# Moving most SBUF tiles of a transformer trunk by 320 bytes, so that matmul operands agree modulo 512

## The chip, the cores and the metric

The kernel runs on one NeuronCore of a Trainium2 chip. The metric is the device time of one execution, in microseconds (us).

## What is computed

The reference is a two-layer decoder trunk over 256 tokens of 2048 features in float32. Layer 0 is a gated DeltaNet block and a squared-ReLU MLP; layer 1 is a differential attention on one shared K/V and a second MLP; each sub-layer ends in `x <- LayerNorm(4**0.25 * x + f(x))`. Cut to what matters here:

```python
D_MODEL, SEQ, D_FF = 2048, 256, 8192

def sq_relu_mlp(x, w_up, w_down):
    return jnp.square(jax.nn.relu(x @ w_up)) @ w_down

def gated_deltanet(x, w_in, conv_w, a_log, dt_bias, norm_w, w_out):
    p = x @ w_in                       # q, k, v, z and two gates
    ...
    return o.reshape(B, S, GDN_V_WIDTH) @ w_out

def diff_attention(x, w_q, lam_params, subln_w, w_o, k_sh, v_sh, lambda_init):
    q = (x @ w_q).reshape(...)
    ...
    return o.transpose(0, 2, 1, 3).reshape(B, S, DIFF_V_WIDTH) @ w_o
```

Nearly all the arithmetic is in the dense products with `w_in`, `w_out`, `w_kv`, `w_q`, `w_o`, `w_up` and `w_down`.

## The kernel before

**The products.** Each dense product is cut into products of 1024 output columns (`gemm`, L117); there are 50 of them. The activations are the stationary operand of TensorE and the weights stream past as the moving operand. Both are split into two parts, hi and lo, kept as float32r, and three passes (hi*hi, hi*lo, lo*hi) give a float32 result. `product` (L166) issues them: for a k-tile of 128 features and a token tile of 128 tokens, on each of two groups of 512 columns, L174 takes `xh` with `wh`, L175 `xh` with `wl`, L176 `xl` with `wh`. A product over 2048 features has 16 k-tiles, 2 token tiles and 2 column groups, so 192 matmuls of 128x128 (stationary) on 128x512 (moving). Each matmul has its own weight load (LDWEIGHTS) of the stationary part.

**Where the stationary operand lies.** Two families. In 30 of the 50 products (all of `w_in`, `w_up`, `w_kv`, `w_q`) it is the features of x in the constant tile `xhl` [128, 2, 2, 16, 128], made at L61 and read by `x_stat` (L110). In the 20 others (`w_out`, `w_down`, `w_o`) it lies in buffers of the pool `blk`, [128, 2048], read by `act_stat` (L114). A stationary part is 128 float32r, 512 bytes in a partition, and all of them follow each other without gaps, so that all parts of a tile start at the same place modulo 512 bytes as the tile. The same holds for the moving parts, 2048 bytes each, in buffers of 4096.

**Weights.** `load_weights` (L154) loads a k-tile of weights by a DMA of SP's queue into `wr`, ScalarE copies it to `wh` (rounded, L78), VectorE subtracts to get `wl` (L79). It runs ahead of TensorE through pools of 4 raw, 6 hi and 6 lo buffers.

**Between the products.** Evacuations, convolutions, the delta rule, attention scores and norms are emitted in units between groups of products (`later`, `soon`, `pump`, L178 to L194). Their transposes to the feature layout (`transpose4`, L200, matmuls of L204 with the identity `ident`) come in groups of four between the products' matmuls. In the DeltaNet stage (products 1 to 8) VectorE carries most of this work.

**Memory.** Constants come first in SBUF, then the pools in the order of L49 to L54 (`raw`, `hi`, `lo`, `blk`, `sm`, `tiny`). One constant, the convolution's taps `cw` (L380), lies behind `ident`, `xhl`, `mask`, `head_w`, `g_after`, `g_ones` and `g_col1` and ahead of `g_beta`, `g_g`, `nlam` and of all the pools.

Of the kernel before, what the change touches and what calls it, by code (L numbers as in the profile page):

```python
# [10 lines left out]
F32 = mybir.dt.float32  # L11
F32R = mybir.dt.float32r
# [6 lines left out]
P = 128  # L19
T = 256  # L20
# [15 lines left out]
class Trunk:  # L36
    """Products run with the activations as the stationary operand and the weights streaming past them.

    Both operands are split exactly into two parts of 12 significant bits (float32r); three passes,
    hi*hi + hi*lo + lo*hi, give a float32 product. Activations for a product are kept with the features  # L40
    on the partitions, [128, (hi, lo), token tile, k-tile, token]; everything else is [token, feature].
    """
# [38 lines left out]
    def rsqrt(self, dst, x, shape):  # L81
        """dst = x ** -0.5 for x > 0 (float32 accuracy: a guess from the exponent and three Newton steps)."""
        v = self.nc.vector
        y, t = self.small(shape, "rsq_y"), self.small(shape, "rsq_t")
        v.tensor_scalar(y.bitcast(I32), x.bitcast(I32), -0.5, float(0x5F3759DF), op0=ALU.mult, op1=ALU.add)
        for i in range(3):
            v.tensor_tensor(t, y, y, op=ALU.mult)
            v.scalar_tensor_tensor(t, t, -0.5, x, op0=ALU.mult, op1=ALU.mult)
            v.scalar_tensor_tensor(dst if i == 2 else y, t, 1.5, y, op0=ALU.add, op1=ALU.mult)

    def rsqrt_column(self, dst, x):
        """rsqrt of a column [128, 1] in fewer steps: (y y x - 3) y, Newton's step less its factor -1/2.

        The guess is scaled by a with -8192 a^27 = 1, which the three factors left out multiply back to 1.
        """
        v = self.nc.vector
        y, t = self.small([1], "rsq_y1"), self.small([1], "rsq_t1")
        a = -(8192.0 ** (-1.0 / 27.0))
        guess = RSQRT_GUESS - 2.0**31
        v.tensor_scalar(y.bitcast(I32), x.bitcast(I32), -0.5, guess, op0=ALU.mult, op1=ALU.add)  # L100
        for i, c in enumerate((3 * a**2, 12 * a**6, 768 * a**18)):
            v.scalar_tensor_tensor(t, y, x, y, op0=ALU.mult, op1=ALU.mult)
            last = v.scalar_tensor_tensor(dst if i == 2 else y, t, c, y, op0=ALU.subtract, op1=ALU.mult)
        return last

    def after(self, ins):
        """What is traced inside takes its turn on the engine of ins behind it."""
        return self.tc.issue_after(ins.ins) if ins is not None else nullcontext()
# [8 lines left out]
    def gemm(self, nk, wsrc, stat, evac, pre=None, rate=1, need=None, cuts=None):  # L117
        """Plans a product: evac(g, t, psum) gets out[token tile t, columns g * 512 ..] of the 1024 columns of wsrc(k)."""
        self.plan.append((nk, wsrc, stat, evac, pre, rate, need, cuts or [SC] * (nk // SC)))

    def run(self):
        steps = [(i, sum(gm[7][:n]), c) for i, gm in enumerate(self.plan) for n, c in enumerate(gm[7])]
        loaded, self.hold = {}, None
        self.load_weights(loaded, *steps[0])
        acc = {}
        for j, (i, s, n) in enumerate(steps):
            nk, _, stat, evac, pre, rate, need, _ = self.plan[i]
            if s == 0:
                acc = {}
                if pre is not None:  # L130
                    pre()
            if need is not None:
                need(s)
            ws = loaded.pop((i, s))
            for t in range(NT):
                # at the end of the second token tile one bank is done before the other, and evacuated meanwhile
                turns = [(g,) for g in range(NG)] if s + n >= nk and t == NT - 1 else [range(NG)]
                for gs in turns:
                    for n_, (k, wh, wl) in enumerate(ws):
                        self.product(acc, k, nk, t, gs, wh, wl, stat)  # L140
                        if n_ and self.pending:
                            fn, args = self.pending.popleft()
                            with self.after(self.last):
                                fn(*args)
                    if s + n >= nk:
                        for g in gs:
                            evac(g, t, acc[g, t])
                if t == 0 and j + 1 < len(steps):
                    with self.after(self.hold):
                        self.load_weights(loaded, *steps[j + 1], self.hold is not None)  # L150
                    self.hold = None
                self.pump(rate)
# [25 lines left out]
    def later(self, fn, *args):  # L178
        """Work on the side of the products: emitted between them, a unit at a time."""
        self.units.append((fn, args))  # L180

    def soon(self, fn, *args):
        """A step of an evac that the tensor engine takes a few products later, when its operand is ready."""
        self.pending.append((fn, args))

    def pump(self, n):
        """Emits n units, and one of the slow chain, whose steps wait for transfers."""
        if self.chain:
            fn, args = self.chain.popleft()
            fn(*args)  # L190
        while n > 0 and self.units:
            fn, args = self.units.popleft()
            fn(*args)
            n -= 1  # L194
# [5 lines left out]
    def transpose4(self, src):  # L200
        """[128, 512] -> PSUM [128, 4, 128], each 128 x 128 block transposed."""
# [5 lines left out]
    def to_features(self, src, dst, t):  # L207
        """src [128 tokens, 512] -> dst [128 features, (hi, lo), token tile, 4, 128 tokens] at token tile t."""
# [17 lines left out]
    def load_x(self, x):  # L226
        """The features of x by quarters: the first at once, the others between the first products."""
# [44 lines left out]
    def ln_finish(self, ln, t, own):  # L272
        """The last normalisation of a token tile: chunks below own on DVE, the others on ACT and Pool beside it."""
# [13 lines left out]
    def residual(self, n, alpha, ln=None):  # L287
        """The evac that adds a product's columns n * 1024 .. to the residual, and normalises it after the last."""
# [26 lines left out]
    def ends(n):  # L315
        """Before a normalisation the first token tile ends early, so that its rows are ready when the second ends."""
        return [5, 5, 6] if n == D // C - 1 else None

    def project_out(self, w, act, g, b, pre=None, need=None, out=None):
        """residual <- LayerNorm(alpha * residual + act @ w)."""  # L320
# [44 lines left out]
    def gated_deltanet(self, x, w_in, conv_w, a_log, dt_bias, norm_w, w_out, g, b, out=None):  # L365
        """The delta rule over all 256 tokens at once, two blocks of 128.

        With k2 = 2 k etc. (silu(y) = (tanh(y / 2) + 1) y / 2), S = |k2|^2 + 4 eps and c = beta / S:
        M = I + strict((k2 k2^T) c_j decay_ij), M y = v sqrt(S) / 2, o = 2 |q2|^-1 dk^-1/2 tril((q2 k2^T) c_j decay_ij) y.
        Matrices are kept transposed, [j, i]; the inverses of M's diagonal blocks are built from 32 x 32 ones.  # L370
        """
# [4 lines left out]
        mask = self.mask  # t <= i  # L376
        after = one.tile([P, P], F32R, name="g_after")  # t > j
        ones = one.tile([P, P], F32R, name="g_ones")
        col1 = one.tile([P, 1], F32, name="g_col1")
        cw = one.tile([P, 4 * 48], F32, name="g_cw")  # L380
# [28 lines left out]
        def gates():  # L409
            """beta = sigmoid(b), g = -exp(a_log) softplus(a + dt_bias) in two parts."""  # L410
# [6 lines left out]
            # the 32 columns four times over: float32r takes a stationary operand of 128  # L417
# [29 lines left out]
            # log(1 + e) = 2 atanh(e / (2 + e))  # L447
# [14 lines left out]
        def conv(raw, h, ct, dst):  # L462
            """Causal convolution and 2 silu of heads h, h + 1 of raw [channel, head, token] to dst [channel, 2, token]."""
# [48 lines left out]
        def score(hf, H, h):  # L512
            """U = (k k^T) c decay and A = (q k^T) c decay of heads h, h + 1, transposed."""
# [43 lines left out]
        def inv_gather(hf):  # L557
            """The 64 diagonal 32 x 32 blocks of the half, one to a partition."""
# [43 lines left out]
        def inv_merge(hf):  # L602
            """Y = the transposed inverses of the 16 128 x 128 blocks, from 32 to 64 to 128."""
# [28 lines left out]
        def solve(hf, gi, H):  # L632
            """Four heads: y, then o and its norm with the norm's weight (the gate follows with z)."""
# [124 lines left out]
    def diff_attention(self, w_kv, w_q, lam_params, subln_w, w_o, g, b, out=None):  # L758
# [27 lines left out]
        def heads(name, follow=None):  # L786
            """The evac that puts a product's heads with the features on the partitions: [128, head, token]."""
# [15 lines left out]
        def prob(hh, h, t, kb):  # L803
            """Where the transposed probabilities of a head's blocks lie: (0, 0), (1, 0), (1, 1)."""
# [3 lines left out]
        def score(kT, qT, hh, h, t):  # L808
            """Heads h, h + 1 of a half, query tile t; the two row tiles of a score go to banks of their own."""
# [40 lines left out]
        def values(hh, gi, t, v):  # L850
            """Four heads: probabilities @ v, the norm of each head, and the features for w_o."""
# [101 lines left out]
```

## Time and profile before

| | before |
|---|---|
| median of 3 runs | 2486.94 us |
| lowest and highest | 2485.38 and 2495.18 us |
| span of the profiled execution (first to last instruction) | 2493.5 us |
| TensorE busy, weight loads busy | 2448.1 us (98%), 1985.4 us (80%) |
| VectorE, ScalarE busy | 1498.4 us (60%), 1078.3 us (43%) |
| DMA | 438.84 MB, mean 176 GB/s |

The profile's page gives the span of the profiled execution and no time beside it. The span is 6.6 us above the median of the runs; of the three runs only the slowest, 2495.18 us, is longer than the span, by 1.7 us.

How to read it: PE is TensorE's matmuls and PEld its weight loads, DVE is VectorE, ACT ScalarE, POOL GpSimd, SP SyncE. A matmul's recorded duration runs from its start to its modelled end and overlaps the next one's, so the distance between two starts is the measure of the pace of the engine, and a row's mean duration is not. [...]

### The profile page before, as it was taken

Reading aid. Unit: us, or ns where it says so; the run is one execution under the profiler, and the core shown is the slowest. Engines: PE = TensorE matmul, PEld = TensorE weight load, DVE = VectorE, ACT = ScalarE, POOL = GpSimd, SP = SyncE. Lnnn points to the kernel's source line nnn. Section 1 sums busy time; section 2 is a strip of 40 time slices with the busy share of each in tenths; the row PEclk is TensorE's granted clock in tenths of the full one; section 3 lists DMA queues with packets and bytes.
Section 4 is the critical chain, followed back from the end, with each engine's and each line's share of the span. In section 5 each row is a group of like instructions: output and inputs, shape, how many; then the busy total and the mean of one; then the engine's idle time right before and its main releaser. Section 6 shows DMA issues by size and latency. Waiting matters only on the chain.

```text
span 2493.5 us, 30465 instructions
## 1 busy us (share of the span) xinstructions
PE 2448.1 (98%) x11492; PEld 1985.4 (80%) x11492; DVE 1498.4 (60%) x2333; ACT 1078.3 (43%) x1474; POOL 89.3 (4%) x94
## 2 busy tenths in 40 slices
PE   8999999999999999999998999999999999999997
PEld 6887888887888888888887877778788888888886
DVE  4789789567554554554557465665755554555556
ACT  4545445333443433434433464653443443443442
POOL 0010010002000000000002000000200000000001
PEclk9999999899999999999999999999999999999999
DMA  6545345464555556565554545454455555656553
GB/s 226 153 136 173 114 133 181 128 235 153 186 182 190 172 199 213 172 211 183 185 197 149 176 137 169 152 170 168 159 195 194 177 186 185 212 176 213 179 194 123
DMA packets 120212, 438.84 MB, mean 176 GB/s; under 512 B 13761, under 2 KB 13793, under 8 KB 119041
## 3 DMA queue, kind: packets, MB, share of 16 engines
q1 hardware_dynamic: 115920, 420.79, 51.2%
q0 software_dynamic: 2560, 11.13, 1.4%
q10 hardware_dynamic: 1584, 4.98, 0.5%
q8 instruction: 90, 1.47, 0.2%
q14 instruction: 58, 0.47, 0.1%
HBM read 433.70 MB, written 3.15 MB: 175 GB/s over the span
## 4 chain that ended last, share of the span: by engine, by line
PE 91%; DVE 5%; DMA 2%; issue 1%; ACT 1%; POOL 0%; SPq 0%; ACTq 0%; POOLq 0%; DVEq 0%
PE acc L175 28%; PE acc L176 28%; PE acc L174 27%; PE ps L204 3%; DVE wl L79 1%; DMA wr<-in_gdn_w_in_dram 1%; DVE blk L266 1%; DVE blk L265 1%; PE ps L818 1%; PE ps L549 1%; ACT wh L78 1%; PE ps L484 0%; DMA wr<-in_mlp_w_up_dram 0%; PE ps L620 0%; PE ps L616 0%
## 5 line engine op out<-in xcount | busy, mean ns | idle before, releaser
L79 DVE TENSOR_TENSOR wl<-wr,wh 128x1024 fp32r<-128x1024 f32 x785 | 954.9, 1227 | 694.3 <-ACT wh L78 671.2
L78 ACT CAST wh<-wr 128x1024 fp32r<-128x1024 f32 x800 | 831.8, 1052 | 969.4 <-PE acc L176 781.2
L174 PE MATMUL acc<-wh,xhl 128*128 128x512 f32 x1920 | 774.2, 403 | 0.1
L175 PE MATMUL acc<-wl,xhl 128*128 128x512 f32 x1920 | 768.5, 400 | 3.7 <-POOL wl L79 2.9
L176 PE MATMUL acc<-wh,xhl 128*128 128x512 f32 x1920 | 764.8, 399 | 0.0
L174 PE MATMUL acc<-wh,blk 128*128 128x512 f32 x1280 | 499.5, 390 | 0.0
L176 PE MATMUL acc<-wh,blk 128*128 128x512 f32 x1280 | 498.9, 390 | 0.0
L175 PE MATMUL acc<-wl,blk 128*128 128x512 f32 x1280 | 498.5, 389 | 0.0
L175 PEld LDWEIGHTS acc<-wl,xhl 128*128 128x128 f32 x1920 | 364.4, 190 | 86.4 <-POOL wl L79 4.2
L174 PEld LDWEIGHTS acc<-wh,xhl 128*128 128x128 f32 x1920 | 364.6, 190 | 84.9 <-issue 1.7
L176 PEld LDWEIGHTS acc<-wh,xhl 128*128 128x128 f32 x1920 | 363.5, 189 | 84.1
L176 PEld LDWEIGHTS acc<-wh,blk 128*128 128x128 f32 x1280 | 240.3, 188 | 50.0
L175 PEld LDWEIGHTS acc<-wl,blk 128*128 128x128 f32 x1280 | 240.4, 188 | 49.5
L174 PEld LDWEIGHTS acc<-wh,blk 128*128 128x128 f32 x1280 | 240.3, 188 | 49.6
L293 DVE SCALAR_TENSOR_TENSOR blk<-blk,acc 128x512 f32<-128x512 f32 x80 | 54.6, 684 | 85.2 <-PE acc L176 85.2
L204 PE MATMUL ps<-ident,sm 128*128 128x128 f32 x512 | 81.1, 274 | 1.4 <-DVE sm L868 1.2
L204 PEld LDWEIGHTS ps<-ident,sm 128*128 128x128 f32 x512 | 62.0, 141 | 24.8 <-PE acc L176 6.7
L78 ACT CAST blk<-ps 128x512 fp32r<-128x512 f32 x80 | 46.9, 586 | 71.3 <-PE ps L204 71.3
L347 DVE TENSOR_TENSOR sm<-sm 128x512 f32<-128x512 f32 x64 | 44.3, 693 | 54.7 <-ACT sm L346 54.3
L79 DVE TENSOR_TENSOR blk<-ps,blk 128x512 fp32r<-128x512 f32 x80 | 55.0, 688 | 30.8 <-ACT blk L78 30.8
L346 ACT ACTIVATE sm<-acc 128x512 f32<-128x512 f32 x64 | 38.3, 599 | 67.7 <-PE acc L176 64.5
L470 DVE SCALAR_TENSOR_TENSOR sm<-blk,g_cw,sm 128x255 f32<-128x255 f32 (+2 forms) x144 | 60.9, 476 | 0.0
(202 smaller groups left out, 1048.4 us busy)
## 6 DMA issues: line engine op xcount, KB each, us to landing
wr<-in_mlp_w_up_dram SPq DMA_DIRECT2D x256, 512.0 KB, 4.7
wr<-in_mlp_w_down_dram SPq DMA_DIRECT2D x256, 512.0 KB, 5.1
wr<-in_gdn_w_in_dram SPq DMA_DIRECT2D x128, 512.0 KB, 4.4
wr<-in_shared_w_kv_dram SPq DMA_DIRECT2D x64, 512.0 KB, 4.9
wr<-in_gdn_w_out_dram SPq DMA_DIRECT2D x32, 512.0 KB, 5.4
wr<-in_diff_w_q_dram SPq DMA_DIRECT2D x32, 512.0 KB, 4.6
wr<-in_diff_w_o_dram SPq DMA_DIRECT2D x32, 512.0 KB, 4.8
blk<-in_ln_g_dram POOLq DMA_DIRECT2D x4, 1024.0 KB, 7.2
```

The source lines that it names most:

```text
L78: self.nc.scalar.copy(hi, src)
L79: (engine or self.nc.vector).tensor_tensor(lo, src, hi.bitcast(F32), op=ALU.subtract)
L174: mm(ps, xh, wh[:, c], start=(k == 0), stop=False)
L175: mm(ps, xh, wl[:, c], start=False, stop=False)
L176: self.last = mm(ps, xl, wh[:, c], start=False, stop=(k == nk - 1))
L204: self.nc.tensor.transpose(pt[:, i], src[:, i * P : (i + 1) * P], self.ident)
L265: v.scalar_tensor_tensor(xc, xc, ln["mv", t][:, 0:1], ln["g"][:, c], op0=ALU.subtract, op1=ALU.mult)
L266: v.scalar_tensor_tensor(xc, xc, ln["rs", t], ln["b"][:, c], op0=ALU.mult, op1=ALU.add)
L293: self.nc.vector.scalar_tensor_tensor(rc, rc, alpha, ps, op0=ALU.mult, op1=ALU.add)
L346: self.nc.scalar.activation(a, ps, AF.Relu)
L347: self.nc.vector.tensor_tensor(a, a, a, op=ALU.mult)
L470: v_.scalar_tensor_tensor(y[:, i, d:], u[:, : T - d], w(j), y[:, i, d:], op0=ALU.mult, op1=ALU.add)
```

## The change

The tile of the taps is made 80 float32 (320 bytes) longer, and only its first 192 columns are used, as before. Comments and docstrings were also taken out, which moves line numbers by at most one.

```diff
-        cw = one.tile([P, 4 * 48], F32, name="g_cw")
+
+        cw = one.tile([P, 4 * 48 + 80], F32, name="g_cw")[:, : 4 * 48]
```

No instruction is added, removed or moved on any engine; shapes and waits are the same. What moves is the start of every tile that lies behind `cw`, by 320 bytes. In the two built programs the tiles start here (bytes in a partition, and the same modulo 512):

| tile | before | mod 512 | with the change | mod 512 |
|---|---|---|---|---|
| `ident` | 16512 | 128 | 16512 | 128 |
| `xhl` | 17024 | 128 | 17024 | 128 |
| `g_after`, `g_ones` | 51328, 51840 | 128 | 51328, 51840 | 128 |
| first `wr` | 53568 | 320 | 53888 | 128 |
| first `wh` | 69952 | 320 | 70272 | 128 |
| first `wl` | 94528 | 320 | 94848 | 128 |
| first `blk` | 119104 | 320 | 119424 | 128 |
| first `sm` | 209216 | 320 | 209536 | 128 |

The buffers of `raw`, `hi`, `lo`, `blk` and `sm` are multiples of 512 bytes long, so all buffers of a pool agree with its first.

## Rows read from the trace of the kernel before

**Rows 1.** Page, parts 1 and 4: busy time by engine; the last chain by engine

```profile
PE 2448.1 (98%) x11492; PEld 1985.4 (80%) x11492; DVE 1498.4 (60%) x2333; ACT 1078.3 (43%) x1474; POOL 89.3 (4%) x94
...
PE 91%; DVE 5%; DMA 2%; issue 1%; ACT 1%; POOL 0%; SPq 0%; ACTq 0%; POOLq 0%; DVEq 0%
```

**Rows 2.** Page, part 5: xcount | busy us, mean ns of one | idle before, releaser

```profile
L174 PE MATMUL acc<-wh,xhl 128*128 128x512 f32 x1920 | 774.2, 403 | 0.1
L175 PE MATMUL acc<-wl,xhl 128*128 128x512 f32 x1920 | 768.5, 400 | 3.7 <-POOL wl L79 2.9
...
L174 PE MATMUL acc<-wh,blk 128*128 128x512 f32 x1280 | 499.5, 390 | 0.0
...
L175 PE MATMUL acc<-wl,blk 128*128 128x512 f32 x1280 | 498.5, 389 | 0.0
```

**Rows 3.** Waits: who <- releaser: us in total, times, longest us

```profile
ACT wh L78 <- PE acc L176: 781.2, 496, 11.4
```

**Rows 4.** Timeline of PE, a product through xhl: start us, us, instruction

```profile
1018.61 0.40 PE L174 MATMUL acc<-wh,xhl 128*128 128x512 f32 x1
...
1039.85 0.39 PE L175 MATMUL acc<-wl,xhl 128*128 128x512 f32 x1
```

**Rows 5.** Timeline of PE, a product through blk

```profile
744.78 0.39 PE L176 MATMUL acc<-wh,blk 128*128 128x512 f32 x1
...
765.86 0.39 PE L176 MATMUL acc<-wh,blk 128*128 128x512 f32 x1
```

**Rows 6.** Windows: four products, two beside DVE's busiest work, then xhl, then blk

```profile
core 0: us, PE busy (x) PEld busy (x) DVE busy (x) ACT busy (x) POOL busy (x), PEclk, DMA share, GB/s
183.60:232.10 48.50, 48.50 (x226) 38.88 (x225) 47.09 (x101) 28.12 (x48) 0.07 (x1) 1.00 0.55 174
371.60:419.70 48.10, 48.10 (x222) 38.60 (x221) 47.62 (x99) 27.74 (x46) 0.00 (x0) 1.00 0.54 176
1004.90:1051.50 46.60, 46.60 (x209) 37.56 (x208) 24.59 (x25) 21.06 (x26) 0.00 (x0) 1.00 0.55 180
...
734.80:778.30 43.50, 43.50 (x193) 36.04 (x192) 21.97 (x21) 16.54 (x17) 0.00 (x0) 1.00 0.56 194
```

**Rows 7.** Line L174: duration ns min/median/max of its matmuls, first and last start

```profile
L174 PE MATMUL acc<-wh,xhl x1920: 388/394/795, 10.6 to 2391.3; 128*128 128x512 f32 x192
...
L174 PE MATMUL acc<-wh,blk x1280: 387/389/481, 497.1 to 2478.9; 128*128 128x512 f32 x183
```

**Rows 8.** Line L424, the gates: the stationary part in blk, the moving one in xhl

```profile
L424 PE MATMUL ps<-xhl,blk x16: 392/397/398, 81.5 to 88.9; 128*128 128x512 f32 x16
```

**Rows 9.** Timeline of PE behind four transposes, a product through xhl

```profile
1007.68 0.60 PE L204 MATMUL ps<-ident,sm 128*128 128x128 f32 x4
1008.03 0.48 PE L174 MATMUL acc<-wh,xhl 128*128 128x512 f32 x1
1008.35 0.39 PE L175 MATMUL acc<-wl,xhl 128*128 128x512 f32 x1
...
1010.21 0.40 PE L174 MATMUL acc<-wh,xhl 128*128 128x512 f32 x1
```

**Rows 10.** The same behind four transposes, a product through blk

```profile
693.53 0.60 PE L204 MATMUL ps<-ident,sm 128*128 128x128 f32 x4
693.89 0.48 PE L174 MATMUL acc<-wh,blk 128*128 128x512 f32 x1
694.21 0.39 PE L175 MATMUL acc<-wl,blk 128*128 128x512 f32 x1
...
696.05 0.39 PE L174 MATMUL acc<-wh,blk 128*128 128x512 f32 x1
```

**Rows 11.** Lines L204 and L857, matmuls of 128 columns: ns min/median/max

```profile
L204 PE MATMUL ps<-ident,sm x512: 270/272/329, 56.9 to 2395.1; 128*128 128x128 f32 x171
...
L204 PE MATMUL ps<-ident,blk x128: 270/273/476, 5.7 to 1771.3; 128*128 128x128 f32 x128
...
L857 PE MATMUL ps<-blk x96: 270/275/275, 1601.8 to 1673.5; 128*128 128x128 f32 x96
```

**Rows 12.** Lines L78 and L79: writes of ACT and DVE to blk and xhl

```profile
L78 ACT CAST blk<-ps x80: 574/587/591, 415.9 to 2395.4; 128x512 fp32r<-128x512 f32 x80
L78 ACT CAST xhl<-ps x32: 579/587/594, 10.0 to 1771.8; 128x512 fp32r<-128x512 f32 x32
...
L79 DVE TENSOR_TENSOR blk<-ps,blk x80: 672/691/693, 417.0 to 2396.5; 128x512 fp32r<-128x512 f32 x80
L79 DVE TENSOR_TENSOR xhl<-ps,xhl x32: 675/684/693, 11.2 to 1772.4; 128x512 fp32r<-128x512 f32 x32
```

## The prediction, made before the changed kernel ran

> **What bounds the kernel now.** I read the busy times and the last chain first [rows 1]: TensorE is busy 98% of the span and holds 91% of the chain that ended last. Then the costliest groups [rows 2]: the products' matmuls come in six groups, three of 1920 with the stationary part in `xhl` (5760 in all) and three of 1280 with it in `blk` (3840). They hardly ever wait; the largest idle time before one of these groups is 3.7 us. The engine that makes their weights waits for TensorE instead: ScalarE sat idle 781.2 us until a matmul of L176 had released a buffer [rows 3]. So TensorE's own pace sets the time, and it is worth looking at what that pace is.
>
> Durations end at a modelled time and overlap, so I took starts from the timeline. In a product through `xhl` without anything between its matmuls, 92 matmuls start between 1018.61 and 1039.85 us: 21.24 us over 91 steps, 233.4 ns a step [rows 4]. In a product through `blk`, 94 start between 744.78 and 765.86 us: 21.08 us over 93 steps, 226.7 ns [rows 5]. [...] The recorded durations say the same: median 394 ns with `xhl`, 389 with `blk` [rows 7]. It is not the evacuation or the DMA: the difference stands in undisturbed stretches, with a DMA share of 0.55 against 0.56.
>
> What differs between the two families is the place of the stationary part. In `xhl` it starts at 128 modulo 512 bytes, while the moving parts in `wh` and `wl` start at 320. In `blk` stationary and moving both start at 320. That is what the change equalises: with it `xhl`, `wh`, `wl` and `blk` all start at 128.
>
> **The change, part by part.** *The longer tile.* 320 bytes in each partition that nothing reads or writes; no instruction is added. Cost 0.
>
> *Products through `xhl`.* If the difference of the starts is what costs the 6.7 ns, all 5760 matmuls could come to the pace of `blk`: 5760 x 6.7 ns = 38.6 us. The bounds of the price come from the durations: 394 - 389 = 5 ns by the medians [rows 7], so 28.8 us; the means (403 and 400 against 390 and 389 [rows 2]) would give 11 ns, but they hold long records behind waits and transposes, which are more frequent in the `xhl` products, so that end is excluded and 6.7 from the starts is taken.
>
> *What that sum leaves out.* Behind a group of transposes the pace has to be found again. In the `blk` product 9 steps from the first matmul behind the transposes took 696.05 - 693.89 = 2.16 us, in the `xhl` product 1010.21 - 1008.03 = 2.18 us [rows 9, 10]. The first step is 0.32 us in both, and over all nine only 0.02 us of 9 x 6.7 = 60 ns shows. So each interruption costs the gain 40 ns. There are 640 transposes in groups of four [rows 11], so 160 groups, and score, value and DeltaNet matmuls between the products besides; nearly all lie in `xhl` products. I take 200 interruptions, an estimate: 200 x 40 ns = 8 us. **38.6 - 8 = 30.6 us.**
>
> *VectorE as cover.* TensorE can only go faster if the weights come faster. In the plain product, the third of [rows 6], VectorE is busy 24.59 and ScalarE 21.06 of 46.60 us: ample. In the second product of the kind that carries the DeltaNet's side work VectorE is busy 47.62 of 48.10 us; TensorE would want 48.10 - 192 x 6.7 ns = 46.8 us, so VectorE is next there and keeps 0.8 us. In the first it is busy 47.09 of 48.50, TensorE would want 47.2: about even. Together I take off 0.8 us. **30.6 - 0.8 = about 30 us.**
>
> *Products through `blk`.* The difference is zero before and after, so nothing changes, if the difference is what counts (the rival below, if not).
>
> *Transposes.* Their moving part `ident` stays at 128 and their source moves from 320 to 128, so here too the starts come to agree. Their median is 272 or 273 ns; L857, whose two parts both lie in `blk`, has 275 at the same 128 columns [rows 11]. So 640 x 3 ns = 1.9 us lost on one side; on the other, nothing shows a gain. I take 0, since the minimum is 270 in all three rows.
>
> *ScalarE, VectorE, DMA at the new places.* Writing to `blk` at 320 and to `xhl` at 128 costs ScalarE 587 ns both times and VectorE 691 and 684 [rows 12]. Their other tiles all move together. I take 0; the work lies beside TensorE's anyway. No transfer of the weights to another place is in the trace; at a DMA share near 0.55 they could take 1.7 times as long before they bounded a product, so 0 as well.
>
> *The sum.* The profiled execution: span 2493.5 us, with the little around it most like the slowest of the three runs (2495.18). Less 30 us its span would be about 2463.5. Nothing in the reduction hangs on that run, so I take it off the median: 2486.94 - 30 = **2457 us**, 1.2% less.
>
> [...] The rows show two paces for one instruction, and the operands' places separate them in every undisturbed stretch that I read. [...] I go by the rows, since I find no other difference between the stretches.
>
> **The rivals.**
> *No change (2487 us).* The 6.7 ns belong to what `xhl` is, not to its start modulo 512: its lower address, or its hi and lo planes 16 KB apart instead of 4. Against it: L175 loads the same `xh` that L174 had just loaded, so the distance of the planes is not met there, and it is as slow as the others (400 against 389 [rows 2]); and in the gates, L424, where `xhl` is the moving part and `blk` at 320 the stationary one, the median is 397 ns, like the disagreeing pairs [rows 8]. For it: the two families are only two tiles, so everything else about them is confounded with the place. Chance 0.10.
>
> *Slower: the place, not the difference, sets the pace (2513 us).* A stationary part at 128 costs 6.7 ns, one at 320 does not. Then `xhl` stays slow and `blk`, which moves to 128, becomes slow: 3840 x 6.7 ns = 25.7 us, with few interruptions to take from it: 2486.94 + 25.7 = 2513. It decides from the point where a pair that agrees at 128 still takes 233 ns. The trace has no such pair. Against it speaks L424 again: its stationary part starts at 320 and it has 397 ns, not 389 [rows 8]; a place alone does not earn the fast pace. But its neighbours are matmuls of 256 columns, so it is weak. Chance 0.07.
>
> *A smaller gain: VectorE becomes the bound in the whole DeltaNet stage (2465 us).* If all eight of its `xhl` products gave back their 1 us, 30 - 8 = 22 us are left. For it: VectorE at 97 to 99% in two of them [rows 6]. Against: the other products show far less, and what is late in one is caught up in the next. Chance 0.05.
>
> *The forecast.* Chance 0.78.
>
> **How the numbers follow.** The forecast's own range: low price 5 ns (28.8 - 8 = 21 us gained, 2466) with 2 us lost on transposes and a few more on VectorE; high, all of 38.6 us without loss at interruptions (2448) and a little for the spread of the runs. The range of 2446 to 2474 holds this and the smaller gain, 0.83 together, and leaves out the other two. What a measurement of this kernel can tell from no change is about 0.5%, 12.4 us. Faster by more than that: the forecast and nearly all of the smaller gain, 0.82. Within it: the no-change rival and a remnant, 0.11. Slower: 0.07.
>
> **What would show it.** In the changed profile the steps of an undisturbed `xhl` product must be 226.7 ns apart, the median of L174 with `xhl` must be 389, the plain `xhl` product (46.60 us before) must last about 45.5, and the `blk` product must stay at 43.50. Paces of 233 in both families would show the rival of the place; 233 and 227 as before the rival of no change; 227 with long waits for `wl` before TensorE's matmuls, in the DeltaNet products, the rival of VectorE. I am wrong in size if the pace falls between 227 and 233, or if interruptions cost another share than I took.

## The result, and the profile after

| | before | with the change |
|---|---|---|
| median of 4 runs each | 2490.09 us | 2464.96 us |
| lowest and highest | 2485.38 and 2495.18 us | 2462.70 and 2467.69 us |
| ratio, 95% interval | | 0.9891, 0.9872 to 0.9909 |
| span of the profiled execution | 2493.5 us | 2463.3 us |
| granted clock, mean of the span | 0.991 | 0.992 |

The granted clock (PEclk on the page) is a share of full speed. The kernel is 1.1% faster by this ratio, 1.0% by the two medians. The two profiled executions differ by 30.2 us. The first page shows where: parts 1, 4 and 5 of the changed kernel's page, beside [rows 1, 2].

```profile
PE 2416.1 (98%) x11492; PEld 1983.3 (81%) x11492; DVE 1497.2 (61%) x2333; ACT 1078.2 (44%) x1474; POOL 90.3 (4%) x94
...
PE 90%; DVE 6%; DMA 2%; issue 1%; ACT 1%; POOL 0%; ACTq 0%; POOLq 0%; DVEq 0%
...
L174 PE MATMUL acc<-wh,xhl 128*128 128x512 f32 x1920 | 764.3, 398 | 0.0
L175 PE MATMUL acc<-wl,xhl 128*128 128x512 f32 x1920 | 757.7, 395 | 3.2 <-POOL wl L79 3.2
...
L174 PE MATMUL acc<-wh,blk 128*128 128x512 f32 x1280 | 500.0, 391 | 0.0
...
L175 PE MATMUL acc<-wl,blk 128*128 128x512 f32 x1280 | 499.1, 390 | 0.0
```

TensorE is busy 32.0 us less, VectorE and ScalarE the same to 1.2 us. The groups through `xhl` lost about 10 us each (774.2 to 764.3, 768.5 to 757.7), the groups through `blk` nothing. The pace itself is in the timeline of PE in the changed kernel: four transposes and the steps behind them, then an undisturbed stretch of a product through `xhl`.

```profile
994.37 0.60 PE L204 MATMUL ps<-ident,sm 128*128 128x128 f32 x4
994.72 0.48 PE L174 MATMUL acc<-wh,xhl 128*128 128x512 f32 x1
...
996.89 0.39 PE L174 MATMUL acc<-wh,xhl 128*128 128x512 f32 x1
...
1004.83 0.39 PE L176 MATMUL acc<-wh,xhl 128*128 128x512 f32 x1
...
1025.91 0.39 PE L176 MATMUL acc<-wh,xhl 128*128 128x512 f32 x1
```

The last two rows are 93 steps apart: 21.08 us, **226.7 ns a step**, the pace that only `blk` had before [rows 4, 5]. Behind the transposes nine steps take 2.17 us, between the 2.18 and the 2.16 of [rows 9, 10].

The windows of the same four products as in [rows 6]:

```profile
core 0: us, PE busy (x) PEld busy (x) DVE busy (x) ACT busy (x) POOL busy (x), PEclk, DMA share, GB/s
181.00:228.90 47.90, 47.88 (x225) 38.81 (x224) 46.97 (x102) 28.11 (x47) 0.28 (x1) 1.00 0.56 177
373.80:422.00 48.20, 47.68 (x221) 38.26 (x220) 47.31 (x100) 27.68 (x46) 0.28 (x1) 1.00 0.55 177
991.60:1037.10 45.50, 45.50 (x209) 37.54 (x208) 24.59 (x25) 21.07 (x25) 0.00 (x0) 1.00 0.56 185
725.10:768.60 43.50, 43.50 (x194) 36.05 (x193) 21.97 (x21) 16.54 (x17) 0.00 (x0) 1.00 0.58 194
```

The plain `xhl` product lasts 45.50 us instead of 46.60, the `blk` product 43.50 as before. The two that carry VectorE's side work gained little: 48.50 to 47.90, and 48.10 to 48.20, where TensorE now waits, as the view of waits in the second one shows (nothing stood there before):

```profile
PE ps L204 <- DVE sm L739: 0.5, 1, 0.5
```

Durations by line (min/median/max ns) in the changed kernel: L174, and L425, which was L424 before and is the gates' matmul with the roles swapped.

```profile
L174 PE MATMUL acc<-wh,xhl x1920: 387/390/796, 11.0 to 2361.2; 128*128 128x512 f32 x192
...
L174 PE MATMUL acc<-wh,blk x1280: 387/389/481, 490.6 to 2448.8; 128*128 128x512 f32 x183
...
L425 PE MATMUL ps<-xhl,blk x16: 389/399/404, 80.3 to 87.6; 128*128 128x512 f32 x16
```

The median through `xhl` fell from 394 to 390 [rows 7], one more than the 389 forecast. That of the gates did not fall: 397 to 399 [rows 8].

### The profile page after: what moved, and what is told of

Its sections match the earlier page's. It is cut to its first block, busy times and chain, and to the rows that moved or that the text cites. A ratio compares the mean times of both kernels' runs of the same rounds, so it can differ in the third digit from the quotient of the medians.

```text
span 2463.3 us, 30465 instructions
## 1 busy us (share of the span) xinstructions
PE 2416.1 (98%) x11492; PEld 1983.3 (81%) x11492; DVE 1497.2 (61%) x2333; ACT 1078.2 (44%) x1474; POOL 90.3 (4%) x94
## 2 busy tenths in 40 slices
DMA packets 120211, 438.84 MB, mean 178 GB/s; under 512 B 13760, under 2 KB 13792, under 8 KB 119040
## 4 chain that ended last, share of the span: by engine, by line
PE 90%; DVE 6%; DMA 2%; issue 1%; ACT 1%; POOL 0%; ACTq 0%; POOLq 0%; DVEq 0%
PE acc L174 27%; PE acc L175 27%; PE acc L176 27%; PE ps L204 3%; DVE wl L79 1%; DVE blk L266 1%; DVE blk L265 1%; PE ps L819 1%; ACT wh L78 1%; PE ps L550 1%; DMA wr<-in_gdn_w_in_dram 1%; PE ps L485 1%; DMA wr<-in_mlp_w_up_dram 0%; PE ps L621 0%; PE ps L847 0%
## 5 line engine op out<-in xcount | busy, mean ns | idle before, releaser
L79 DVE TENSOR_TENSOR wl<-wr,wh 128x1024 fp32r<-128x1024 f32 x785 | 954.5, 1227 | 675.0 <-ACT wh L78 632.1
L78 ACT CAST wh<-wr 128x1024 fp32r<-128x1024 f32 x800 | 832.1, 1052 | 945.6 <-PE acc L176 757.2
L174 PE MATMUL acc<-wh,xhl 128*128 128x512 f32 x1920 | 764.3, 398 | 0.0
L175 PE MATMUL acc<-wl,xhl 128*128 128x512 f32 x1920 | 757.7, 395 | 3.2 <-POOL wl L79 3.2
L176 PE MATMUL acc<-wh,xhl 128*128 128x512 f32 x1920 | 754.8, 393 | 0.0
L174 PE MATMUL acc<-wh,blk 128*128 128x512 f32 x1280 | 500.0, 391 | 0.0
L174 PEld LDWEIGHTS acc<-wh,xhl 128*128 128x128 f32 x1920 | 363.8, 189 | 73.8 <-issue 1.7
L174 PEld LDWEIGHTS acc<-wh,blk 128*128 128x128 f32 x1280 | 240.4, 188 | 49.5
L204 PE MATMUL ps<-ident,sm 128*128 128x128 f32 x512 | 81.3, 275 | 2.5 <-DVE sm L869 1.8
L204 PEld LDWEIGHTS ps<-ident,sm 128*128 128x128 f32 x512 | 61.3, 140 | 27.3 <-PE acc L176 7.1
L78 ACT CAST blk<-ps 128x512 fp32r<-128x512 f32 x80 | 46.8, 585 | 70.9 <-PE ps L204 70.9
L79 DVE TENSOR_TENSOR blk<-ps,blk 128x512 fp32r<-128x512 f32 x80 | 55.0, 688 | 30.1 <-ACT blk L78 30.1
```

Source lines behind the costliest of these rows:

```text
L78: self.nc.scalar.copy(hi, src)
L79: (engine or self.nc.vector).tensor_tensor(lo, src, hi.bitcast(F32), op=ALU.subtract)
L174: mm(ps, xh, wh[:, c], start=(k == 0), stop=False)
L175: mm(ps, xh, wl[:, c], start=False, stop=False)
L176: self.last = mm(ps, xl, wh[:, c], start=False, stop=(k == nk - 1))
L204: self.nc.tensor.transpose(pt[:, i], src[:, i * P : (i + 1) * P], self.ident)
```

## Experiments

Theory D says that the difference of the two starts sets the pace; theory P that the place of one operand does; theory R that the two families differ by something else.

### Two probes of the pace

A kernel that only streams matmuls, each pair of starts on a line of its own, with four transposes between the pairs. Shortened, with `s` and `m` for the starts of the stationary and the moving operand in bytes:

```python
for i in range(60):
    mm(ps[i // 3 % 2], S[:, s // 4 + i // 2 % 2 * 128 :][:, :128], M[:, m // 4 :][:, :512], start=True, stop=True)
apart()     # four transposes
```

> A probe that leaves out the whole computation of the reference: 60 matmuls in a row for each pair of starts (stationary, moving, in bytes modulo 512), float32r 128x128 on 128x512 unless said, groups divided by four transposes. Theory D (only the difference of the two starts modulo 512 counts): about 227 ns a step at difference 0 wherever both lie (0/0, 320/320, 128/128, 64/64, 16/16), about 233 at 128/320 and every pair with the same difference (320/0), other differences open but equal for equal differences. Theory P (the place of one operand counts): 128/128 not at 227, or 320/128 equal to 320/320. Theory R (the two families differ by something else than the starts): one pace for all pairs. A pair below 227 would be a better layout for the kernel.

The timeline of PE in this probe shows three steps to a row, and the two rows given of each line are 27 steps apart. L75 is 0/0, L89 192/0, L93 256/0, L111 128/320 (the kernel before, through `xhl`), L115 128/128 (the changed kernel):

```profile
23.63 0.84 PE L75 MATMUL acca<-M,S 128*128 128x512 f32 x3
...
29.75 0.85 PE L75 MATMUL accb<-M,S 128*128 128x512 f32 x3
...
124.37 0.85 PE L89 MATMUL acca<-M,S 128*128 128x512 f32 x3
...
130.55 0.85 PE L89 MATMUL accb<-M,S 128*128 128x512 f32 x3
...
152.93 0.84 PE L93 MATMUL acca<-M,S 128*128 128x512 f32 x3
...
159.05 0.85 PE L93 MATMUL accb<-M,S 128*128 128x512 f32 x3
...
282.09 0.86 PE L111 MATMUL acca<-M,S 128*128 128x512 f32 x3
...
288.39 0.86 PE L111 MATMUL accb<-M,S 128*128 128x512 f32 x3
...
310.44 0.84 PE L115 MATMUL acca<-M,S 128*128 128x512 f32 x3
...
316.56 0.84 PE L115 MATMUL accb<-M,S 128*128 128x512 f32 x3
```

6.12 us over 27 steps is 226.7 ns, 6.18 is 228.9, 6.30 is 233.3. All pairs whose starts are multiples of 64, read in the same way from the second half of each series:

| stationary minus moving, modulo 256 | pairs (stationary/moving) | ns a step |
|---|---|---|
| 0 | 0/0, 256/0, 0/256, 64/64, 128/128, 320/320 | 226.7 |
| 64 | 64/0, 320/0, 128/320, 0/192, 0/448 | 233.3 |
| 128 | 128/0, 384/0 | 232.3 |
| 192 | 192/0, 448/0, 320/128, 0/64 | 228.9 |

So the difference counts and the place does not, as theory D says, with two things that it did not say: it counts **modulo 256**, not 512, and it has a sign: 192 costs 2.2 ns, 64 costs 6.7. P and R are out for these steps. Nothing else runs beside the series (from 20 to 320 us VectorE is busy 0.00 us and the DMA share is 0.00), so the traffic of other engines does not make the paces either. The probe cannot show whether anything else in the kernel hangs on the places.

A second probe let the starts alternate from step to step, took shorter moving operands and set groups of 6 to 48 steps between transposes.

> A second probe that leaves out the computation of the reference. Steps whose starts alternate: first (stationary, moving) 0/0 and 64/64 in turn, then 64/0 and 0/64 in turn, the same with 128. Theory O (a matmul is slowed by its own pair's difference): the first series at 226.7 ns a step, the second at the mean of 233.3 and 228.9, that is 231. Theory N (the running matmul's moving stream is slowed by the weight load of the next matmul): the other way round, the first series at 231 and the second at 226.7; with 128 the first at 232.3 and the second at 226.7. Further: starts shifted by 4 to 48 bytes, where a difference below 64 bytes counts either like 0 (rounded down to a multiple of 64) or not; moving operands of 256 and 384 columns, where 256 gave 120.0 at difference 0 and 117.8 at 64 before, the other way than 512; and groups of 6 to 48 steps between transposes at difference 0 and 64: by the 40 ns an interruption that the prediction took off, a group of 6 gains nothing, one of 24 gains about 120 ns and one of 48 about 280 ns.

Neither theory on the pair held. With 0/0 and 64/64 in turn the step is 231.6 ns, with 64/0 and 0/64 in turn 231.7; with 128 in place of 64 it is 228.4 and 230.0. Theory O wanted 226.7 in the first series and N in the second. So the agreement of each pair is not enough where the starts change from step to step; which weight load's start counts for a step, its own or a later one's, stays open.

The groups came out as the 40 ns wanted. In the timeline of this probe, rows of the four transposes, with 24 steps between them: the first three rows at difference 0, the last two at 64.

```profile
450.06 0.60 PE L70 MATMUL pt<-ident,Sf 128*128 128x128 f32 x4
455.99 0.60 PE L70 MATMUL pt<-ident,Sf 128*128 128x128 f32 x4
461.91 0.60 PE L70 MATMUL pt<-ident,Sf 128*128 128x128 f32 x4
...
474.32 0.60 PE L70 MATMUL pt<-ident,Sf 128*128 128x128 f32 x4
480.35 0.60 PE L70 MATMUL pt<-ident,Sf 128*128 128x128 f32 x4
```

A group of 24 takes 5.93 us at difference 0 and 6.03 at 64, 0.10 to 0.11 us less where 24 x 6.7 would be 0.16: an interruption costs the gain about 50 ns. Groups of 6 take 1.48 us in both cases, so there next to nothing is gained, and groups of 48 differ by about 0.28 us of 0.32, which makes it 40 ns.

### The whole kernel at other places

Five variants of the whole kernel, and the changed one once more. Everything agreeing at 320: `xhl` moved by 192 bytes, the pools by 512.

```diff
+        self.const.tile([P, 48], F32, name="gap")
         self.xhl = self.const.tile([P, 2, NT, KD, P], F32R, name="xhl")
...
-        cw = one.tile([P, 4 * 48], F32, name="g_cw")
+        cw = one.tile([P, 4 * 48 + 80], F32, name="g_cw")[:, : 4 * 48]
```

> Everything agrees, but at 320 instead of 128: xhl moved by 192 bytes, the pools by 512. Theory D: as the changed kernel, 2465 us within 5, steps through xhl and blk 226.7 ns. Theory P (128 is the good place): xhl or blk slower, 2476 us or more. Theory R (xhl gained because it or the weights' pools moved): not 2465 unless any move would do.

The changed kernel with `blk` (and `sm`) pushed away from the weights:

```diff
+        self.gap = pool("gap", 1)
+        self.gap.tile([P, 48], F32, name="gap")
         self.blk_pool = pool("blk", 11)
```

> The changed kernel with blk and sm pushed 192 bytes on: xhl and the weights agree at 128, blk lies at 320. Theory D: the xhl steps stay at 226.7 ns, the blk steps go to 230 to 236 (the difference is +192 here and was -192 for xhl before), so up to 3840 x 6.7 ns = 26 us more, 2485 to 2491 us. Theory P (a stationary part at 320 is as good as one at 128): blk stays at 226.7, 2465 us.

The changed kernel again, and the tile longer by 64, 128 and 192 bytes instead of 320 (the last two with `+ 32` and `+ 48`):

```diff
-        cw = one.tile([P, 4 * 48 + 80], F32, name="g_cw")[:, : 4 * 48]
+        cw = one.tile([P, 4 * 48 + 16], F32, name="g_cw")[:, : 4 * 48]
```

> The changed kernel once more, as the measure for the three beside it: both theories 0.989 of the kernel before, steps of 226.7 ns through xhl and blk.

> The tile is 64 bytes longer instead of 320, so the pools start at 384 and xhl stays at 128: difference 256. Theory 256 (the difference of the starts counts modulo 256, as the probe had it): as the changed kernel, 0.989, xhl steps 226.7 ns. Theory 512 (they must agree modulo 512, as the change says): xhl steps above 229 ns, 0.993 or more.

> 128 bytes longer: pools at 448, difference 192 modulo 256 for xhl. Theory 256 with the probe's paces: xhl steps 228.9 ns instead of 233.3, so 5760 x 4.4 = 25 us less some 3 for the interruptions, about 22 us gained, 0.991. A theory in which only agreement helps: no gain, 1.00.

> 192 bytes longer: pools at 0, difference 128 for xhl. Theory 256 with the probe's paces: xhl steps 232.3 ns, 5760 x 1.0 = 6 us gained, 0.998. A theory in which any move of the pools helps (their start at a multiple of 512): 0.989.

What was measured, with differences modulo 256, steps from undisturbed stretches of the timelines (86 to 93 steps), and span times mean granted clock. Span and clock are those of the one profiled execution of each kernel; the clock is rounded to 0.001, which leaves about 1 us in the last column:

| kernel | difference for `xhl`, `blk` | step `xhl`, `blk`, ns | ratio to before, interval | span, us | clock | span x clock |
|---|---|---|---|---|---|---|
| before | 64, 0 | 233.4, 226.7 | 1 | 2493.5 | 0.991 | 2471 |
| changed | 0, 0 | 226.7, 226.7 | 0.9891, 0.9872 to 0.9909 | 2463.3 | 0.992 | 2444 |
| changed, again | 0, 0 | 226.7, 226.7 | 0.988, 0.9851 to 0.991 | 2471.9 | 0.988 | 2442 |
| all at 320 | 0, 0 | 226.6, 226.6 | 0.991, 0.9874 to 0.9946 | 2457.9 | 0.994 | 2443 |
| 64 bytes | 0, 0 | 226.7, 226.7 | 0.9913, 0.9887 to 0.9939 | 2482.7 | 0.983 | 2440 |
| `blk` apart | 0, 192 | 226.6, 229.0 | 0.9925, 0.9898 to 0.9951 | 2469.5 | 0.993 | 2452 |
| 128 bytes | 192, 0 | 228.9, 226.7 | 0.9917, 0.989 to 0.9943 | 2466.8 | 0.994 | 2452 |
| 192 bytes | 128, 0 | 232.3, 226.7 | 0.998, 0.9959 to 1.0002 | 2489.9 | 0.989 | 2463 |

The steps are those of the probe in every case. The intervals of the ratios overlap in all the changed kernels but the one of 192 bytes, so it is the steps and the last column that tell them apart, not the runs' times. Three timelines as they stand, of PE. First 64 bytes, a product through `xhl`, 89 steps in 20.18 us:

```profile
1145.96 0.39 PE L175 MATMUL acc<-wl,xhl 128*128 128x512 f32 x1
...
1166.14 0.39 PE L174 MATMUL acc<-wh,xhl 128*128 128x512 f32 x1
```

128 bytes, a product through `xhl`, 88 steps in 20.14 us:

```profile
1128.09 0.39 PE L175 MATMUL acc<-wl,xhl 128*128 128x512 f32 x1
...
1148.23 0.39 PE L176 MATMUL acc<-wh,xhl 128*128 128x512 f32 x1
```

`blk` apart, a product through `blk`, 88 steps in 20.15 us:

```profile
1047.44 0.39 PE L178 MATMUL acc<-wh,blk 128*128 128x512 f32 x1
...
1067.59 0.39 PE L176 MATMUL acc<-wh,blk 128*128 128x512 f32 x1
```

The recorded durations would have hidden this last one. The median of that kernel's L177 (`wl` with `blk`) is 388 ns, no more than with agreeing starts, though the steps are 2.3 ns longer. A duration ends at a modelled time; only starts show the pace.

```profile
L177 PE MATMUL acc<-wl,blk x1280: 387/388/478, 486.8 to 2455.3; 128*128 128x512 f32 x183
```

What follows: 64 bytes more do what 320 do, so agreement modulo 512 is not needed, only modulo 256; agreement at 320 is as good as at 128 by steps and last column, though the median of its runs, 2472.45 us, missed the "2465 us within 5" that I expected. 128 bytes gain most of it (19 of 27 us by the last column), 192 bytes little (8 us; the interval of its runs includes no change at all). `blk` apart fell short of what I expected (2485 to 2491 us; its runs have a median of 2472.96): theory D did not know the sign of the difference and I gave +192 the price of -192 (64), 26 us; the step grew by 2.3 ns, 3840 x 2.3 = 8.8 us, and the column of span times clock shows 8 (2452 against 2444).

### What makes single executions differ

The spans scatter more than the steps do: the 64-byte kernel has the same steps as the changed one and a span 19.4 us longer. The granted clock says why. In some stretches, mostly in the DeltaNet stage and in the last 10 us or so of the span, it is 0.50 (mean 0.66 in the last 13.5 us of the kernel before and 0.59 in the last 13.3 us of the changed one, where TensorE is busy 0.00 us). A window of 20.5 us of the kernel before:

```profile
456.80:477.30 20.50, 20.50 (x143) 16.45 (x140) 5.50 (x7) 4.42 (x6) 0.00 (x0) 0.50 0.29 99
```

One of the changed kernel:

```profile
267.90:288.40 20.50, 20.50 (x128) 16.42 (x127) 5.63 (x6) 5.19 (x7) 0.00 (x0) 0.50 0.32 99
```

The 64-byte kernel has two of them:

```profile
268.10:288.60 20.50, 20.50 (x128) 16.32 (x126) 5.64 (x6) 5.46 (x7) 0.00 (x0) 0.50 0.30 91
462.60:483.10 20.50, 20.50 (x137) 16.44 (x134) 4.95 (x6) 4.41 (x6) 0.00 (x0) 0.50 0.26 86
```

What such a stretch costs is in the timeline of PE in the window of the kernel before:

```profile
458.24 0.63 PE L175 MATMUL acc<-wl,xhl 128*128 128x512 f32 x1
458.67 0.63 PE L176 MATMUL acc<-wh,xhl 128*128 128x512 f32 x1
459.10 0.63 PE L174 MATMUL acc<-wh,xhl 128*128 128x512 f32 x1
```

A step takes 0.43 us there, against 233.4 ns at clock 1.00. So where TensorE is the bound, a stretch at half the clock costs about half its length (46% by these two paces), and span times mean clock is an estimate of what an execution would take without them. It bears this out: the spans of the four executions with agreeing starts lie up to 24.8 us apart, the products within 4 us, and the others follow in the order of what their steps cost. In the 10 us ahead of the stretch TensorE was busy for 9.59 us in the kernel before and all 10 in the changed one, at clock 1.00; what starts such a stretch was not tried.

## Why the prediction was right

The forecast was 2457 us in a range of 2446 to 2474, 30 us less; measured were 2464.96, and 25.1 us less by the medians (22.7 to 31.9 by the interval of the ratio, 30.2 between the profiled executions, of which about 3 are the clock's by span times clock, so 27). Of the 8 us between 2457 and 2464.96, about 3 come from the kernel before alone: with its fourth run its median is 2490.09, and the forecast was taken off 2486.94. By its steps:

- **The pace of the products through `xhl`** was right: 226.7 ns now, from 233.4, both at a granted clock of 1.00 (the windows of the plain product), so 6.7 ns a step as taken from the starts; the bound of 11 ns by the mean durations was rightly left out. That difference, and not a place, sets it is shown by the first probe and by everything agreeing at 320. The period was taken as 512 bytes and is 256; that cost the forecast nothing, since the change makes the starts equal.
- **The interruptions** were right: 40 ns each were taken off, the second probe shows 40 to 50. Their number, 200, was an estimate; in the trace, of either kernel, TensorE comes back from other matmuls to a product through `xhl` 209 times.
- **VectorE as cover** was a little too small. I took off 0.8 us for two products. Without VectorE each would have gained about 1.0 us (192 x 6.7 ns less eight or so interruptions); they gained 0.6 and lost 0.1, so 1.5 us are missing there, worked out from the windows. About 0.5 of it is this execution's: in the changed kernel run again, with all at 320 and with 64 bytes the second product lasted 47.7 us. With that the sum closes: 38.6 less 209 x 45 ns less 1.5 is 27.7 us, against the 27 of span times clock. The rival in which the whole stage gives its gain back did not come: the stretch of its seven products behind the first fell from 434.7 to 429.2 us. Some of that is the clock's (0.97 and 0.98 in the two stretches), but the second, third and sixth product, at 1.00 in both, fell from 56.3 to 55.5, 64.9 to 64.1 and 64.8 to 64.1 us.
- **Products through `blk`** stayed at 226.7 ns and 43.50 us a product, as said; the rival of the place is refuted.
- **ScalarE, VectorE, DMA**: the casts and subtractions of the weights take 1052 and 1227 ns as before; the median of the transposes stayed at 272 and 273 ns; the DMA moved 438.84 MB in both. All at 0, rightly.
- **One argument did not hold.** I used the gates (L424) against two rivals: their pair disagreed and had 397 ns. With agreeing starts they have 399. Their steps alternate between 512 and 256 columns, and by the starts one of each together takes 353.6 ns in both kernels. So they do not show what a stream of equal steps shows, and the argument read a recorded duration where only starts tell the pace. The rivals were wrong, but not for that reason.
- **How far it reaches.** For float32r with 512 columns the pace hangs on the start of the stationary operand relative to that of the moving one (226.7 against 233.3 ns). Why the two starts matter, no run shows. For bfloat16 with 512 columns the first probe has one pace, 215.8 ns at the six pairs of starts tried, and for plain float32 with 256 columns one too (215.8 ns between records, two to a matmul, at both pairs tried).

## What to carry to other kernels

When one instruction of one shape runs at two paces, compare the starts of its records, not their durations, and look at the addresses of its operands; here 64 bytes of padding in an unrelated tile were worth 0.9% (0.6 to 1.1%), and 320 bytes 1.1%. For float32r products of 512 columns, put the starts of stationary and moving operands at multiples of 64 bytes that agree modulo 256 (226.6 to 226.7 ns a step in the runs, 228.9 to 233.4 where they differ), all of them in the same way (231.6 with 0/0 and 64/64 in turn), and estimate the gain as steps times the difference of the paces less 40 to 50 ns for each interruption of the stream. For another type or number of columns, measure it first, since the sign can turn (with 256 columns 120.0 ns at difference 0 and 113.3 at 64).

## What the runs showed that I had not expected

- The period is 256 bytes, and the cost is not symmetric: 228.9 ns at a difference of 192, 233.3 at 64, 232.3 at 128.
- With a moving operand of 256 columns agreement is the slowest: 120.0 ns a step at difference 0, 118.7 at 128, and 113.3 at 64 and 192. In the second probe's timeline (27 steps between the rows of a line), L117 is difference 0 and L119 is 64. In the first probe, where the stationary part changes only at every second step, 256 columns at 320/0 took 117.8, so at this width the difference modulo 256 does not settle the pace alone. With 384 columns it is 173.3 at 0 and 192, 175.6 at 128 and 176.7 at 64.

```profile
306.45 0.52 PE L117 MATMUL acca<-M,S 128*128 128x256 f32 x3
...
309.69 0.52 PE L117 MATMUL accb<-M,S 128*128 128x256 f32 x3
...
313.90 0.50 PE L119 MATMUL acca<-M,S 128*128 128x256 f32 x3
...
316.96 0.51 PE L119 MATMUL accb<-M,S 128*128 128x256 f32 x3
```

- Even at its best a float32r step of 512 columns takes 226.7 ns, 10.9 more than a bfloat16 one (215.8). No pair of starts that was tried got below that.
- Starts that are no multiples of 64 differ again: with the moving operand at 0, a stationary one at 16, 32 or 48 costs 233.3 ns, at 96 234.3, and at 240 or 496 (16 short of agreement) 226.7. Two operands at 16 agree and still take 233.3 in the first probe and 230.0 in the second, where two at 32 take 226.7.
